# Modulation columns in steps of two weight tiles, begun one convolution pair later; chunk B's first norm in steps of two tiles

## The chip, the cores and the metric

The kernel runs on one core of one Trainium2 chip. The metric is device time in microseconds (us). Three runs of the kernel before took 1693.92, 1695.59 and 1695.64 us; the median is 1695.59 us. The profile shows one execution on the same core.

The engines are named as in the profile: PE is TensorE (PEld its weight loads), DVE is VectorE, ACT is ScalarE, POOL is GpSimd and SP is SyncE, which here issues DMAs only.

## The reference

A trunk of two layers on `x` of 1024 positions by 1024 channels, all in f32. Each layer normalises, modulates, mixes tokens, adds, and does the same around a feed-forward. The modulation comes from one vector `c`:

```python
c_act = jax.nn.silu(c)
for i in range(DEPTH):
    mod = c_act @ ada_w[i] + ada_b[i]
    sh_m, sc_m, g_m, sh_f, sc_f, g_f = jnp.split(mod, N_ADA, axis=-1)
    h = modulate(rms_norm(x, norm_mix_g[i]), sh_m, sc_m)
    ...
    x = x + (1.0 + g_m)[:, None, :] * y
    h = modulate(rms_norm(x, norm_ffn_g[i]), sh_f, sc_f)
    y = swiglu_ffn(h, ffn_w_gate[i], ffn_w_up[i], ffn_w_down[i])
    x = x + (1.0 + g_f)[:, None, :] * y
```

Layer 0 mixes by a Conformer convolution: a product to 2048 channels with a gate, a causal depthwise convolution of 31 taps, a layer norm over the channels, silu, and a product back. Layer 1 mixes by trailing means. The change is in layer 0 alone: in the vectors `g_m`, `sh_f`, `sc_f` and `g_f` of its modulation (numbered `j` = 2 to 5), and in the norm ahead of its convolution.

## The kernel before

**Tiling.** Channels lie on the 128 partitions, so 1024 channels are `KT` = 8 tiles; the 1024 positions are two chunks, A and B, of 512. Every large product is done in three parts (high by high, high by low, low by high, in `fp32r`), so one output tile of 128 channels by 512 positions takes 8 x 3 = 24 products of PE. It fills a PSUM bank, of which the tag `mm` has six.

**Order on PE.** PE executes its instructions in the order in which the Python code emits them; the other engines are ordered by a scheduler. The work stands in a list of units (`unit`, run by `run_units`). A unit emits products and calls `pace()` at fixed places: in `conv_in` after every 12 products (every 6 with `fine=2`), in the taps after every 12, in `conv_out` once behind a unit of 24. Behind each unit there is a further `pace()`, which adds nothing to PE's clock.

**The planner.** `clock` holds a planned time for PE, VectorE, GpSimd and ScalarE. `matmul` adds `n / 2400 + 0.0025` for an `fp32r` product of `n` columns and four times the first part for f32, so 12 products of 512 add 2.59. `pace()` steps the tasks that are due: first those that are urgent or `free`, then the others for as long as VectorE's or GpSimd's clock is less than 4 ahead of PE's. A task is a generator; what it yields says when it is next due. A key of `LOAD` is due so much PE clock later; `"spread"` is due 3.0 behind the later of VectorE's and ScalarE's clocks. `finish(task)` steps a task to its end and passes over what is due.

**The modulation columns.** `ada_columns(js)` (line 447) computes `js` = (2, 3) and later (4, 5), 16 weight tiles of 128 x 1024 f32 (512 KB) each time. For one tile `k` of vector `j` four products (32 columns wide, side by side in the array) take the silu of `c` as the stationary operand and the tile's four quarters as the moving one, and add to one PSUM bank. Their f32 takes two records each in the profile, eight a tile. After `k` = 7 `columns_done` copies the bank with ScalarE, yields `"spread"`, turns the row into columns with two small products (`adac`), adds the bias on VectorE and makes the gains on GpSimd. The tiles come over SP's queue into two buffers (`ADA_BUFS`); a load waits until the products that read its buffer have run. For `j = 3`, if `held[0]` is set, the turning is put off (`held_back`) to behind the first unit of `conv_out(A)`.

**Order of the units around it.** `ada_first` begins columns 2 and 3. Then stand the beginning of chunk B's norm (`norm_first`); the taps of A's pairs 0 to 3; `conv_in` for A's pairs 4 and 5, each with two banks, `a` and `g`; one unit for A's pairs 6 and 7, `finish` of B's norm, and B's 6 and 7 with the same weights; B's pairs 0 and 1; the taps that PE does itself (`pe_taps`, 46 taps, 138 products, in groups of eight whose units end at 24, 45, 69, 93, 117 and 138 products). Then:

```python
    unit(lambda take: held.__setitem__(0, True))
    unit(lambda take: finish(T["ada", 0]))
    unit(lambda take: finish(*(T["taps", 0, p] for p in range(KT) if PE_TAPS.get(p, 0) < CW)))
```

and `ada_second`, which begins columns 4 and 5; B's pairs 2, 3 and 4, beside which A's layer norm runs (products `mean`, `var` and `rstd` on PE, its sums and `v` on VectorE); `conv_out(A)` with eight units named `y`; `scale_done`, which forces `j = 4` if it isn't there; B's pair 5 beside A's norm for the feed-forward; and the feed-forward's products `p`. Behind eight of their units `first_head` finishes columns 4 and 5.

**The norm.** `norm` (line 648) takes the root of the mean of squares (`mean_rsqrt`: products `var`, small VectorE steps, products `rstd`) and then steps through the eight tiles. `modulated` emits for each tile a VectorE operation `t`, the high part `h` on ScalarE and the low part `h` on VectorE. Between two steps `pace()` may emit taps: GpSimd's and ScalarE's (`pa`, `pr`), or VectorE's (`ca`).

Of the kernel before, what the change touches and what calls it, by code (L numbers as in the profile page):

```python
# [19 lines left out]
KT = D // P  # L20
# [24 lines left out]
ADA_BUFS = 2  # L45
# [6 lines left out]

PE_TAPS = {6: 15, 7: CW}
DIAGS = 8
LOAD = {"load": 4.0, "slow": 6.0, "next": 4.0, "dots": 4.0}

ON_DVE = (1, 4)
AHEAD = 4
# [4 lines left out]
LOADED = 4  # L63
SPLIT = 2
STRAIGHT = 1
BESIDE = 12
HOLD_TAPS = 4
STRETCH = 1.2
# [63 lines left out]
def trunk(ctx, tc, xT, c, vec, ada, adan, w1f, w1, wdg, w2, wgu, wdn, wds, wpl, out):  # L132
    nc = tc.nc
    ctx.enter_context(tc.manual_schedule(engines={mybir.EngineType.PE}))
    clock = {"PE": 0.0, "V": 0.0, "G": 0.0, "S": 0.0}
# [10 lines left out]
    def matmul(out, lhsT, rhs, start, stop, more=False):  # L146
        n = out.shape[-1]
        clock["PE"] += n / 2400 * (1 if rhs.dtype == F32R else 4) + 0.0025
        last_mm[0] = nc.tensor.matmul(out, lhsT, rhs, start=start, stop=stop, skip_group_check=more).ins.name  # L149
# [55 lines left out]
    def nm(s):  # L205
        uid[0] += 1
        return f"{s}_{uid[0]}"
# [9 lines left out]
    def step(t, e):  # L217
# [8 lines left out]
        if V_.spent > before["V"] and isinstance(t, Taps) and t.ch.i:  # L226
            beside.append(V_.last.ins)
            del beside[:-BESIDE]
        for k in "VG":
# [26 lines left out]
    class Task:  # L256
# [6 lines left out]
        def step(self, e):  # L263
            if e != "V" or self.done or clock["PE"] < self.until and not forced[0]:
                return False
            try:
# [3 lines left out]
                if said == "wait":  # L270
                    return False
                if said in LOAD:
                    self.until = clock["PE"] + LOAD[said]
                elif said == "root":
# [12 lines left out]
    def block(tag, name, dt=F32R):  # L287

        pool, bufs = (raws, RAW_BUFS if tag == "raw" else ADA_BUFS) if tag in ("raw", "ada") else (slots, KT if tag[0] == "h" else KT // 2)
        return pool.tile([P, 2, 512], dt, tag=tag, name=nm(name), bufs=bufs)  # L290
# [15 lines left out]
    def bank(name):  # L306
        return ps.tile([P, 512], F32, tag="mm", name=nm(name))
# [64 lines left out]
    ccols = cst.tile([P, KT, 32], F32, name="ccols")  # L372
# [22 lines left out]
    def ada_load(src, queue=sync):  # L395
        w = raws.tile([P, D], F32, tag="ada", name=nm("adaw"), bufs=ADA_BUFS)
        queue.dma_start(w, src)
        return w
# [45 lines left out]
    Q = D // 4  # L444

    def ada_columns(js):


        todo = [(j, k) for j in js for k in range(KT)]
        src = lambda j, k: adan[k, :, (j - 2) * D : (j - 1) * D]  # L450
        ws = [ada_load(src(*t)) for t in todo[:ADA_BUFS]]
        for i, (j, k) in enumerate(todo):
            yield "load"
            if k == 0:
                acc = bank("ada")
            w = ws.pop(0)
            for g in range(4):
                matmul(acc[32 * g : 32 * g + 32, :Q], ccols[:, k, :], w[:, g * Q : g * Q + Q], start=k == 0, stop=k == KT - 1)
            clock["PE"] -= 1.3
            if i + ADA_BUFS < len(todo):  # L460
                ws.append(ada_load(src(*todo[i + ADA_BUFS])))
            if k == KT - 1 and (j != 3 or not held[0]):
                yield from columns_done(j, acc)
            elif k == KT - 1:
                held_back.append((j, acc))
# [3 lines left out]
    def columns_done(j, acc):  # L469

        rows = temp(Q)
        S_.copy(rows, acc[:, :Q])
        yield "spread"
        cols = bank("adac")
        for h in range(2):
            matmul(cols[:, 4 * h : 4 * h + 4], rows[:, h * P : h * P + P], quarters, start=True, stop=True)
        m = mod[:, j * KT : (j + 1) * KT]
        V_.tensor_tensor(m.rearrange("p (q h) -> p q h", h=2), cols[:, :KT].rearrange("p (h q) -> p q h", h=2),
                         V("ada_b", j * KT, KT).rearrange("p (q h) -> p q h", h=2), op=ADD)
        ada_gains(0, j, 0, KT, G_)  # L480
        ada_done.add((0, j))
# [148 lines left out]
    def rms(ch, keep=False):  # L630
        acc = yield from sum_sq(x[ch.i], ch.n)
        return (yield from mean_rsqrt(acc, ch.n, keep))
# [19 lines left out]
    def norm(ch, l, ffn, key, keep=False, squares=None):  # L652
        blocks = [block(f"h{ch.i}", "h") for _ in range(KT)]
        h = st[key] = [(b[:, 0], b[:, 1]) for b in blocks]
        st["blocks", ch.i] = blocks
        if squares is not None:
            rstd = yield from mean_rsqrt(squares.acc, ch.n, keep, loose=ch.i and not l)
        else:
            rstd = yield from rms(ch, keep)
        quiet[0] = ffn and not l  # L660
        for k in range(KT):
            if k == HOLD_TAPS:
                quiet[0] = False
            modulated(ch, l, ffn, h, rstd, k)
            yield


    units = []
# [1 line left out]
    def unit(emit, *weights):  # L670
        units.append((weights, emit))
# [36 lines left out]
    def conv_u(ch, p):  # L708
        u = st["u", ch.i, p] = wslot(ch, "u", p)
        if ch.i == 0:  # L710
            G_.memset(u[:, :HALO], 0.0)
        else:
            G_.tensor_copy(u[:, :HALO], uhalo[:, p, :])
        return u
# [20 lines left out]
    def conv_in(*todo, fine=4):  # L735

        def emit(take):
            got = {}
            for each in todo:
                if each is None:  # L740
                    finish(T["norm_b"])
                    continue
                ch, p = each
                conv_u(ch, p)
                wts = got.setdefault(p, [])
                b = [bank("a"), bank("g")]
                for i in range(2):
                    if len(wts) == i:
                        wts.append(take())
                    for k in range(KT):  # L750
                        products(b[i], wts[i], k, st["h", ch.i][k], k == 0, k == KT - 1)
                        if k % fine == fine - 1:
                            pace()
                conv_glu(ch, p, *b, fine < 4)
                if ch.i == 0 and PE_TAPS.get(p, 0) < CW:
                    T["taps", 0, p] = Taps(A, p)
                if ch.i == 0 and p == KT - 1:
                    for q in PE_TAPS:
                        if PE_TAPS[q] < CW:
                            split_u(q)  # L760
        tiles = list(dict.fromkeys(e[1] for e in todo if e))
        unit(emit, *[w1[p, i] for p in tiles for i in range(2)])
# [818 lines left out]
    def ending(ch, l):  # L1581
# [40 lines left out]
        def emit(parts):  # L1622
            behind_it = iter(())
            for s, (o, n) in enumerate(ENDS):
                last, straight = s == len(ENDS) - 1, []
                acc = st["upper"][:, o : o + n]
                for d in range(KT // 2):
# [7 lines left out]
                    S_.activation(sq, xs, AF.Square)  # L1635
                    if last and d > STRAIGHT:
                        straight.append(sq)
# [53 lines left out]
    for k in range(KT):  # L1691
# [4 lines left out]
        if k > 1:  # L1696
            acc = squares[0]
# [16 lines left out]
    w = ada_pair(0)  # L1714
# [7 lines left out]
    for k in range(KT + 1):  # L1722
        if k < KT:
            if k:
                w = ada_pair(k)
# [3 lines left out]
                dots = [V_.last.ins]  # L1729
# [8 lines left out]
        if k < KT:  # L1738
# [7 lines left out]
            t = temp(A.n) if k else first_t  # L1746
# [48 lines left out]
    def ada_first(take):  # L1795
        T["ada", 0] = Task(ada_columns((2, 3)), False, 0)
        T["ada", 0].free = True
    unit(ada_first)
    def norm_first():
        squares = Squares(B, True)  # L1800
        for k in range(KT + 1):
# [7 lines left out]
    taps(A, *range(FIRST))  # L1809
    for p in range(FIRST, KT - 1 - SHARE):  # L1810
        conv_in((A, p))
    some = range(KT - 1 - SHARE, KT)
    conv_in(*[(A, p) for p in some], None, *[(B, p) for p in some])
    put("ln_a", lambda: layer_norm_silu(A), True)
# [227 lines left out]
```

## Time and profile before

| What | us |
|---|---|
| median of three runs | 1695.59 |
| the profiled execution | 1694.43 |
| its span in the profile | 1692.7 |
| PE busy | 1665.5 |
| columns 2 and 3 on PE, first to last tile | 71.64 to 173.63 |
| columns 4 and 5 on PE, first to last tile | 206.14 to 323.01 |
| the 32 tiles' own products on PE | 20.4 |
| chunk B's norm: `rstd` on PE | 101.58 |
| first product of B's pair 6, which reads that norm | 118.37 |

All times but the first two are counted from the start of the span, which is 1.7 us shorter than the execution. A line of the timeline gives the start, the time taken, the engine, the source line, the operation, `out<-in` by the program's names, the operand's shape and the count of merged instructions, and in brackets the engine's idle time before it with what ended that. `L149` and `L126` are the helpers that emit all products and all vector operations, so the tiles' names tell the work: `ada<-adaw,ccols` is a modulation tile, `a` and `g` are the banks of a convolution pair, `tap` the taps on PE, and `first` the first four pairs.

### The profile page before, as it was taken

The page shows a single profiled execution, that of the slowest core. Times are in us where ns is not written, and L with a number is a line of the kernel's source. Part 1 is how long each engine was busy: PE and PEld are TensorE (multiplying, and loading weights), DVE is VectorE, ACT ScalarE, POOL GpSimd, SP SyncE. Part 2 cuts the span into 40 slices and gives each one's busy share as a digit, 9 for nine tenths or more (in the row PEclk, how much of TensorE's full clock was granted, in tenths as well). Part 3 has the DMA queues.
Part 4 walks back from the last instruction along what each step waited for, and adds up shares of the span by engine and source line. Part 5 has one row for each costly group of instructions (what it writes and reads, how often), then busy time and mean ns, then how long its engine had stood idle before and what let it go on. Part 6 is the DMA issues. An engine that isn't in the chain of part 4 may idle for free.

```text
span 1692.7 us, 21280 instructions
## 1 busy us (share of the span) xinstructions
PE 1665.5 (98%) x7586; PEld 1356.0 (80%) x7586; DVE 1318.3 (78%) x1872; ACT 799.7 (47%) x1085; POOL 489.6 (29%) x566
## 2 busy tenths in 40 slices
PE   7999999999999999999999999999999999999997
PEld 5777777778887888888888888888888888888887
DVE  8889899899758887888665797848877677668656
ACT  3679686866546332333213436646422222234344
POOL 3587767796001111212110222100111111000013
PEclk9999999999999999999999999999999999999999
DMA  8958987828675789886878846877677776677564
GB/s 302 289 173 234 231 232 200 224 78 238 216 237 155 257 261 298 271 265 212 339 266 285 260 146 202 245 243 212 175 231 230 213 221 193 203 269 206 190 168 125
DMA packets 115884, 380.70 MB, mean 225 GB/s; under 512 B 12289, under 2 KB 14465, under 8 KB 115778
## 3 DMA queue, kind: packets, MB, share of 16 engines
q1 hardware_dynamic: 78464, 247.99, 41.6%
q0 software_dynamic: 36736, 130.83, 31.6%
q8 instruction: 60, 0.98, 0.2%
q10 hardware_dynamic: 578, 0.53, 0.1%
q14 instruction: 46, 0.38, 0.1%
HBM read 311.92 MB, written 63.18 MB: 222 GB/s over the span
## 4 chain that ended last, share of the span: by engine, by line
PE 87%; DVE 6%; DMA 2%; issue 2%; ACT 2%; POOL 1%; DVEq 0%; SPq 0%; ACTq 0%; POOLq 0%
PE a L149 24%; PE dn L149 23%; PE e L149 13%; PE p L149 12%; PE y L149 6%; PE g L149 3%; PE first L149 3%; PE tap L149 2%; POOL pa L126 1%; PE ada L149 1%; DVE t L126 1%; DMA adaw<-in_adan_dram 1%; DVE x L126 1%; PE var L149 1%; DVE w L126 1%
## 5 line engine op out<-in xcount | busy, mean ns | idle before, releaser
L126 ACT CAST w<-raw 128x1024 fp32r<-128x1024 f32 (+1 forms) x249 | 258.8, 1042 | 329.8 <-PE dn L149 93.6
L149 PE MATMUL dn<-g,w 128*128 128x512 f32 x1152 | 265.3, 390 | 1.6 <-DVE g L126 1.0
L149 PEld LDWEIGHTS dn<-g,w 128*128 128x128 f32 x1152 | 215.5, 188 | 48.0 <-DVE g L126 1.3
L126 DVE TENSOR_TENSOR w<-raw,w 128x1024 fp32r<-128x1024 f32 (+1 forms) x177 | 217.7, 1233 | 42.8 <-ACT w L126 42.4
L149 PE MATMUL a<-n,w 128*128 128x512 f32 x1056 | 247.7, 390 | 1.1 <-DVE n L126 0.7
L149 PE MATMUL p<-h,w 128*128 128x512 f32 x1056 | 244.2, 390 | 0.8 <-DVE h L126 0.6
L126 POOL TENSOR_TENSOR pa<-pa,pr 128x512 f32<-128x512 f32 x160 | 229.6, 1521 | 23.3 <-ACT pr L126 17.1
L149 PEld LDWEIGHTS a<-n,w 128*128 128x128 f32 x1056 | 197.8, 188 | 44.2 <-DVE n L126 2.2
L149 PEld LDWEIGHTS p<-h,w 128*128 128x128 f32 x1056 | 197.3, 188 | 43.8 <-DVE h L126 1.5
L149 PE MATMUL dn<-hi,w 128*128 128x512 f32 (+1 forms) x600 | 173.7, 373 | 0.8 <-DVE w L126 0.8
L126 DVE SCALAR_TENSOR_TENSOR ca<-u,vecs,ca 128x512 f32<-128x512 f32 x245 | 169.7, 746 | 0.5
L126 DVE SCALAR_TENSOR_TENSOR x<-dn,gains,x 128x512 f32<-128x512 f32 (+1 forms) x144 | 100.8, 729 | 35.7 <-PE dn L149 35.4
L149 PEld LDWEIGHTS dn<-hi,w 128*128 128x128 f32 x600 | 109.7, 188 | 20.9 <-DVE w L126 1.3
L149 PE MATMUL a<-t,w 128*128 128x512 f32 x528 | 123.5, 389 | 0.8 <-DVE w L126 0.8
L149 PE MATMUL e<-b,w 128*128 128x512 f32 x528 | 123.4, 389 | 0.6 <-DVE r L126 0.6
L149 PE MATMUL e<-t,w 128*128 128x512 f32 x528 | 123.3, 389 | 0.0
L126 ACT ACTIVATE pr<-u,vecs 128x512 f32<-128x512 f32 x160 | 108.2, 716 | 25.5 <-POOL pa L126 17.4
L1119 POOL DMA_DIRECT2D raw<-in_wgu_dram x41 | 36.3, 886 | 285.7 <-DVE k L126 89.8
L149 PEld LDWEIGHTS a<-t,w 128*128 128x128 f32 x528 | 99.0, 188 | 21.8 <-DVE w L126 1.2
L149 PEld LDWEIGHTS e<-b,w 128*128 128x128 f32 x528 | 99.0, 188 | 21.6 <-DVE r L126 1.0
L149 PEld LDWEIGHTS e<-t,w 128*128 128x128 f32 x528 | 99.1, 188 | 20.6
L149 PE MATMUL dn<-lo,w 128*128 128x512 f32 (+1 forms) x300 | 111.7, 372 | 0.0
(183 smaller groups left out, 2374.3 us busy)
## 6 DMA issues: line engine op xcount, KB each, us to landing
raw<-in_wgu_dram SPq DMA_DIRECT2D x132, 512.0 KB, 4.9
adaw<-in_ada_dram POOLq DMA_DIRECT2D x48, 512.0 KB, 7.4
raw<-in_wdn_dram SPq DMA_DIRECT2D x44, 512.0 KB, 7.8
raw<-in_wgu_dram POOLq DMA_DIRECT2D x41, 512.0 KB, 7.0
raw<-in_w_dram SPq DMA_DIRECT2D x36, 512.0 KB, 6.1
gd<-g POOLq DMA_DIRECT2D x36, 512.0 KB, 7.8
g<-gd SPq DMA_DIRECT2D x36, 512.0 KB, 5.5
kinds<-k POOLq DMA_DIRECT2D x33, 512.0 KB, 7.2
```

The costliest lines, as they stand in the source:

```text
L126: self.last = self.order(getattr(self.eng, name)(out, *args, **kw))
L149: last_mm[0] = nc.tensor.matmul(out, lhsT, rhs, start=start, stop=stop, skip_group_check=more).ins.name
L1119: d = order(nc.gpsimd.dma_start(w[i], wgu[l, fp, src], accum_op=ADD))
```

## The change

Three things change. `ada_columns` takes its tiles by twos: it waits once, does the eight products of two tiles one after the other, and then issues the loads of the next two together. It is due 16.0 of PE's clock after its beginning (`"first"`) and 11.0 after each step (`"both"`), where it was 4.0 for each tile (`"load"`); a pair's net price in PE's clock falls from 2 x (1.717 - 1.3) to 2 x (1.717 - 1.465). The unit `ada_first` moves from ahead of B's norm to behind A's pair 4. And `norm` yields after every second tile for chunk B in layer 0, so that two tiles are emitted in one step.

```diff
-LOAD = {"load": 4.0, "slow": 6.0, "next": 4.0, "dots": 4.0}
+LOAD = {"load": 4.0, "both": 11.0, "first": 16.0, "slow": 6.0, "next": 4.0, "dots": 4.0}
...
+WHEN = 4
...
         ws = [ada_load(src(*t)) for t in todo[:ADA_BUFS]]
-        for i, (j, k) in enumerate(todo):
-            yield "load"
-            if k == 0:
+        for i in range(0, len(todo), ADA_BUFS):
+            yield "both" if i else "first"
+            these = todo[i : i + ADA_BUFS]
+            if these[0][1] == 0:
                 acc = bank("ada")
-            w = ws.pop(0)
-            for g in range(4):
-                matmul(acc[32 * g : 32 * g + 32, :Q], ccols[:, k, :], w[:, g * Q : g * Q + Q], start=k == 0, stop=k == KT - 1)
-            clock["PE"] -= 1.3
-            if i + ADA_BUFS < len(todo):
-                ws.append(ada_load(src(*todo[i + ADA_BUFS])))
+            for (j, k), w in zip(these, ws):
+                for g in range(4):
+                    matmul(acc[32 * g : 32 * g + 32, :Q], ccols[:, k, :], w[:, g * Q : g * Q + Q], start=k == 0, stop=k == KT - 1)
+                clock["PE"] -= 1.465
+            ws = [ada_load(src(*t)) for t in todo[i + ADA_BUFS : i + 2 * ADA_BUFS]]
             if k == KT - 1 and (j != 3 or not held[0]):
                 yield from columns_done(j, acc)
...
             modulated(ch, l, ffn, h, rstd, k)
-            yield
+            if not ch.i or l or k % 2:
+                yield
...
-    unit(ada_first)
...
         conv_in((A, p))
+        if p == WHEN:
+            unit(ada_first)
```

## The prediction

> **What bounds the kernel now.** I read the page first, then the waits of TensorE (PE) in the first 330 us, where all the changed code runs, then PE's timeline there.
>
> ```profile
> PE 1665.5 (98%) x7586; PEld 1356.0 (80%) x7586; DVE 1318.3 (78%) x1872; ACT 799.7 (47%) x1085; POOL 489.6 (29%) x566
> PE var L149 <- DVE acc L126: 5.8, 1, 5.8
> ...
> PE p L149 <- DVE h L126: 0.6, 2, 0.3
> PE ada L149 <- DMA adaw<-in_adan_dram: 0.6, 1, 0.6
> PE y L149 <- DVE v L126: 0.5, 1, 0.5
> ```
>
> PE is busy for 98% of the span, and after the first 20 us its waits (waited for, total, times, longest) are tenths. So PE's instruction list is the clock of the kernel: what leaves that list is gained and what enters it is paid, unless the list then meets a wait. Three such places stand close by: the modulation tile that waited 0.6 us for its DMA, the first `y` unit (0.5 us for VectorE's `v`), and the first `p` units (0.6 us for `h`).
>
> **One tile, and two in one step.** Today each weight tile is a step of its own behind 24 products.
>
> ```profile
> 91.03 0.64 PE L149 MATMUL ada<-adaw,ccols 128*32 128x256 f32 x8 [0.60 <-DMA adaw<-in_adan_dram]
> 91.59 1.05 PE L149 MATMUL var<-ones,acc 128*128 128x1 f32 x8
> ...
> 101.58 1.05 PE L149 MATMUL rstd<-ident,col 128*128 128x128 f32 x8
> ...
> 117.80 0.64 PE L149 MATMUL ada<-adaw,ccols 128*32 128x256 f32 x8
> 118.37 5.74 PE L149 MATMUL a<-h,w 128*128 128x512 f32 x24
> 123.95 0.50 PE L149 MATMUL adac<-quarters,t 128*128 128x4 f32 x4
> 124.31 5.69 PE L149 MATMUL g<-h,w 128*128 128x512 f32 x24
> ```
> ```profile
> 247.62 5.68 PE y L149 x24
> 253.30 0.57 PE ada L149 x8
> 253.87 16.55 PE y L149 x72
> ```
> ```profile
> L149 PE MATMUL ada<-adaw,ccols x256: 379/391/403, 71.6 to 323.3; 128*32 128x256 f32 x128
> ...
>   issue: 11.0, 31
> ```
>
> Both `y` runs of the chain follow a tile, so 48 more products cost 16.55 - 5.68 = 10.87, 0.2265 us each. 24 then need 5.44, and 5.68 holds 0.24 of restart. A tile costs 0.57 + 0.24 = 0.81 us. The x256 are 8 records a tile: 32 tiles, 25.9 us. The eight run in two rounds; 0.64 of busy time less 0.39 for the last one leaves 0.25 between rounds. The last row is weight loads sitting idle before tiles, 11.0 us in 31 times, 0.35 each: the list empties at the change of shape. In a pair the second tile has the same shape, so I give it two rounds, 0.50, and none of the emptying: a pair is 0.81 + 0.50 = 1.31, and 16 pairs save 16 x 0.31 = 5.0 us. No row shows two tiles in a row. At the dear end the second pays the full 0.81 (gain 0); at the cheap end its rounds hide in the first's 0.39 tail, 0.39 less each, 11.2 in all. I take 0.31, nearest to the rows of one tile.
>
> [...]
>
> **Where the pairs fall.** The kernel places steps by its own PE clock. 12 products add 2.59 to it and end in a look at what is due; a pair adds 0.50, `var` 0.02, `rstd` 0.86. Zero is the end of A's pair 4, where the loads are now begun. The first step is due at 16.0 and comes at 18.15 (half of A6's `g`). Each next is due 11.0 behind: 29.87 (half of A7's `g`), 43.33 (end of B6), 56.78 (half of B0's `a`). That ends shift `j = 2`; its turning into columns waits by the clocks of VectorE and ScalarE, three looks (7.8), 65.07. The fifth is then due at 76.07, just past the end of B1 (75.43), and falls 12 products into the taps (78.0), the sixth at 69 (90.6), the seventh, due at 102.06, misses the look at 117 products (101.1) and comes at 129 of 138. The eighth isn't due at all: `finish(T["ada", 0])` forces it at 138. Its two tiles can be fetched only when the seventh has left the two buffers. **So nine products separate a pair from the loads of the next**, where the loads used to have a whole bank. One look less for the columns gives 21 products, one more gives none.
>
> **Up to the forced pair.**
>
> ```profile
> 173.63 0.64 PE L149 MATMUL ada<-adaw,ccols 128*32 128x256 f32 x8
> 174.20 7.75 PE L149 MATMUL tap<-us,w 128*128 128x496 f32 x33
> 181.79 0.51 PE L149 MATMUL adac<-quarters,t 128*128 128x4 f32 x4
> 182.15 18.61 PE L149 MATMUL tap<-us,w 128*128 128x508 f32 x81
> 200.60 5.61 PE L149 MATMUL a<-h,w 128*128 128x512 f32 x24
> 206.14 0.64 PE L149 MATMUL ada<-adaw,ccols 128*32 128x256 f32 x8
> 206.71 1.13 PE L149 MATMUL mean<-acc,ones 128*128 128x512 f32 x2
> ```
>
> Before 200.60 go: 16 tiles, 12.96; the DMA wait, 0.60, since early pairs are 11 units apart; the second `adac`, 0.36 (123.95 to 124.31), which moves behind the first `y`. Seven pairs, 9.17, come. Gain 4.75: the taps end at 195.85 and the seventh pair 9 x 0.2265 = 2.04 earlier, at 193.8.
>
> ```profile
> 192.77 0.33 SPq L491 DMA_DIRECT2D raw<-in_w_dram  x1
> 193.15 1.01 SPq L167 DMA_DIRECT2D adaw<-in_adan_dram  x2
> ```
> ```profile
> DMA to landing us min/median/max: 8.5/9.6/10.8
> ```
> ```profile
> DMA to landing us min/median/max: 3.4/5.9/12.4
> ```
> ```profile
> 0.00:20.00 20.00, 8.38 (x21) 5.01 (x21) 12.83 (x28) 10.11 (x17) 2.77 (x38) 1.00 0.91 347
> ```
>
> SP issues two at 193.15 today, in this very stretch, behind a weight load; they land 8.5 and 10.8 us after issue. The third row is all 32 loads; 3.4 alone plus 512 KB at the best rate seen, 347 GB/s, 1.5, makes 4.9 the short end, 10.8 the long one. I take 8.0, between them, as the change's weight load comes about 2 us sooner and is half done. On SP nothing but the next weight loads queues behind these two, five tiles ahead of PE. The second is issued by 194.4 and lands at 202.4; 0.5 later the pair is done, 202.9 (199.8 to 205.7). PE waits some 6 us. With 5.54 for the bank, `mean` begins at 208.4 (205.3 to 211.2) against 206.71: **1.7 us late** (1.4 early to 4.5 late).
>
> **From there to the end.**
>
> ```profile
> 203.99 1.49 DVE L126 TENSOR_TENSOR acc<-acc,u 128x512 f32<-128x512 f32 x2
> ...
> 228.36 4.87 DVE L126 TENSOR_TENSOR u<-u,rstd 128x512 f32<-128x512 f32 x8 [0.17 <-PE rstd L149]
> ...
> 245.58 0.68 DVE L126 TENSOR_TENSOR v<-t,v 128x512 fp32r<-128x512 f32 x1
> ```
> ```profile
> 301.66 0.64 PE L149 MATMUL ada<-adaw,ccols 128*32 128x256 f32 x8
> ```
>
> Columns 4 and 5 begin at the same place as before, their first step due 16 later. Between `mean` and `var` one pair replaces two tiles, +0.31; between `var` and `rstd` one tile goes, +0.81. From `rstd` to the last product of the first `y`, VectorE works 228.36 to 246.26 without a hole, so a saving there only lengthens the 0.5 us wait: 0. Behind it 10 tiles and two `adac` (8.82) become 6 pairs and three (8.94), -0.12. The tile at 301.66 stood ahead of the `h` waits and no pair replaces it there: they grow, -0.81. Sum +0.2. After 340 us nothing is edited, and PE's list is what it was.
>
> **Chunk B's norm.** Its root is one look later (end of A6's `g`), because PE's clock lacks the old steps; in time that is 101.2 against 101.58.
>
> ```profile
> L126 DVE SCALAR_TENSOR_TENSOR h<-t,mod,h 128x512 fp32r<-128x512 f32 x8 | 9.7, 1224 | 0.0
> L126 DVE SCALAR_TENSOR_TENSOR t<-x,gains,rstd 128x512 f32<-128x512 f32 x8 | 5.7, 737 | 2.7 <-PE rstd L149 2.7
> ...
> L126 DVE SCALAR_TENSOR_TENSOR u<-a,vecs,t 128x512 f32<-128x512 f32 x1 | 0.7, 739 | 0.0
> ...
> L126 DVE SCALAR_TENSOR_TENSOR uhalo<-a,vecs,t 128x30 f32<-128x30 f32 x1 | 0.2, 230 | 0.0
> ```
>
> That is VectorE from the root's columns (102.7) to the norm's end (122.75): 20.1 us, 15.4 of them the norm's sixteen operations, the rest gating and taps. B6 starts at 118.37 now; with two pairs ahead in place of eight tiles, and the DMA wait gone, at 113.9. It reads the last tile 21 products in, 4.8 later, 118.7: 17.5 behind the root, whose spreading takes 0.9. Two tiles at a time put four at the root and two at each of the next steps, so little but the gating (0.9) can stand between: 16.3 of 16.6, no cost. If as much stands between as today, PE waits 20.1 + 0.9 - 17.5 = 3.5; that end stays in the range. The taps put off are still due only at the taps' `finish`.
>
> **What else moves.**
>
> ```profile
> 129.49 7.46 ACT L126 ACTIVATE x<-x,gate_b 128x512 f32<-128x512 f32 x12
> ```
>
> Shift `j = 2` ends some 25 us later in PE's list, and with it POOL's two small gains and this block on ScalarE, which needs them. Behind it queue the sigmoids that free PE's banks; PE has one bank's time, 5.5, in hand, so 0 to 2.0, and I take 0, as no wait on PE followed it here. The first two loads leave SP's queue at 62 and come about 12 us later, where 4 loads fewer are in flight by 98; PE waited for none but its tile, so 0. The accumulator of `j = 3` stays in its bank past the taps; if the six run out, a bank's release by VectorE costs tenths to 1 us. The smaller price in the clock gives VectorE some 5 us less planned work by 340 us, all of it due later.
>
> **Sum.** 1.7 - 0.2 = 1.5 us slower. The profiled execution took 1694.43 (span 1692.7), 1.2 under the median of 1695.59; I add to the median: **1697.1**, no change that can be seen.
>
> **Rivals.** *The forced pair costs nothing* (it is reached later than I count, or its loads land at once). PE would be at `mean` at 195.85 + 1.31 + 5.54 = 202.7, where VectorE's `acc` ended at 205.48 and can come earlier only by what it idled: gain 1.2 to 4.0, with the 0.2 a time of 1691.4 to 1694.2. For it: three steps miss the look before by 0.64 of the clock alone, so one term that I left out undoes the replay. Against: the same count puts the old tiles where the trace has them, one behind each 24 products. *PE runs slow after the wait*, the other side:
>
> ```profile
> 11.88 1.87 PE L149 MATMUL var<-ones,acc 128*128 128x1 f32 x8 [5.85 <-DVE acc L126]
> ```
> ```profile
> 19.28 4.94 PE L149 MATMUL first<-h,w 128*128 128x512 f32 x12 [1.65 <-ACT h L126]
> ```
>
> After 5.85 us idle the eight `var` took 1.87 us where 1.05 is the rule, and 12 products took 4.94 against 2.72: 2.2 lost, though the granted clock of that stretch reads 1.00. A wait of 6 us at 196 would be like it; 1.5 + 2.2 = 3.7 slower, 1699.3. [...] *The pair saves nothing*: seven pairs put the forced load 2.2 later and the rest adds 2.5: 6.2 slower, 1701.8.
>
> **Chances.** A measurement tells 0.2%, 3.4 us, from no change. Forecast 0.51 (1694.0 to 1699.9 by the loads, to 1703 with a wait at B6: 0.02 faster, 0.37 same, 0.12 slower); free forced pair 0.30 (0.17 faster, 0.13 same); slow PE 0.12 (0.05 same, 0.07 slower); no saving 0.07 (0.01 same, 0.06 slower). Together 0.19, 0.56, 0.25. The range, 1691.2 to 1702.5, leaves out the ends of the outer cases.
>
> **What would show it.** Right: groups of 16 `ada` products about 0.5 longer than 0.64; none with a DMA wait before 130 us; a wait for `adaw` of 4 to 9 us right behind the last tap; a longer wait of the first `y`. Wrong: an eighth pair without a wait, `mean` before 205, `var` or taps slowed behind the wait, or B6's `a` waiting for `h`.

## The result: 1.8% slower, and the profile after

The changed kernel takes 1726.12 us (median of six runs, 1725.01 to 1729.54) against 1695.75 for the kernel before in the same job: ratio 1.0181, 95% interval 1.0171 to 1.0192. The prediction, 1697.1 with a range to 1702.5, missed by 29 us; "slower" had been given 0.25. The profiled execution took 1725.4, its span is 1723.6.

The engines' shares on the page show nothing of it: PE still has 97%.

```profile
PE 1672.0 (97%) x7586; PEld 1366.4 (79%) x7586; DVE 1317.7 (76%) x1872; ACT 802.3 (47%) x1088; POOL 487.9 (28%) x566
```

PE's waits between 60 and 370 us do (waited for: total, times, longest). Before, the rows of this view that lie in the edited stretch came to 1.7 us (`p` 0.6, `ada` 0.6, `y` 0.5).

```profile
PE ada L150 <- DMA adaw<-in_adan_dram: 6.0, 2, 5.2
PE adac L150 <- ACT t L127: 4.7, 1, 4.7
PE y L150 <- ACT t L127: 4.6, 1, 4.6
PE rstd L150 <- DVE col L127: 4.3, 1, 4.3
PE p L150 <- ACT t L127: 2.6, 1, 2.6
PE g L150 <- ACT t L127: 1.6, 2, 1.4
PE a L150 <- DVE h L127: 1.6, 2, 0.8
PE p L150 <- DVE h L127: 1.3, 2, 0.9
```

That is 26.7 us, 25.0 more than before. PE's timeline of the changed kernel shows what each wait leaves behind:

```profile
107.39 2.05 PE L150 MATMUL rstd<-ident,col 128*128 128x128 f32 x8 [4.30 <-DVE col L127]
...
109.10 7.37 PE L150 MATMUL a<-h,w 128*128 128x512 f32 x24
116.30 2.88 PE L150 MATMUL g<-h,w 128*128 128x512 f32 x12
119.11 1.07 PE L150 MATMUL ada<-adaw,ccols 128*32 128x256 f32 x16
120.12 3.06 PE L150 MATMUL g<-h,w 128*128 128x512 f32 x12
123.01 4.47 PE L150 MATMUL a<-h,w 128*128 128x512 f32 x19
...
142.78 5.60 PE L150 MATMUL g<-h,w 128*128 128x512 f32 x24
148.22 2.88 PE L150 MATMUL a<-h,w 128*128 128x512 f32 x12
...
203.49 1.07 PE L150 MATMUL ada<-adaw,ccols 128*32 128x256 f32 x16
...
211.96 1.08 PE L150 MATMUL ada<-adaw,ccols 128*32 128x256 f32 x8 [5.20 <-DMA adaw<-in_adan_dram]
213.84 1.08 PE L150 MATMUL ada<-adaw,ccols 128*32 128x256 f32 x8 [0.81 <-DMA adaw<-in_adan_dram]
214.85 4.65 PE L150 MATMUL a<-h,w 128*128 128x512 f32 x12
219.34 1.02 PE L150 MATMUL mean<-acc,ones 128*128 128x512 f32 x2
...
259.51 7.28 PE L150 MATMUL y<-v,w 128*128 128x512 f32 x24 [4.63 <-ACT t L127]
271.45 1.01 PE L150 MATMUL adac<-quarters,t 128*128 128x4 f32 x4 [4.67 <-ACT t L127]
272.32 7.63 PE L150 MATMUL y<-v,w 128*128 128x512 f32 x24
...
354.69 4.61 PE L150 MATMUL p<-h,w 128*128 128x512 f32 x12 [2.58 <-ACT t L127]
```

Three things are to be seen. **The pairs cost what was forecast**: from 116.30 to 123.01 lie 24 products and a pair, 6.71; 24 products alone take 148.22 - 142.78 = 5.44; a pair is 1.27 (forecast 1.31). **The eighth pair waited as forecast**, 5.20 + 0.81 = 6.0. **And after each long wait the products run slow**: `rstd` 2.05 for 1.05, `a` 7.37 for 5.60, half a bank 4.65 for 2.88, `y` 7.28 and 7.63 for 5.60, `p` 4.61 for 2.88. The forced pair itself takes 2 x 1.08 where a pair has 1.07. That is 1.0 + 1.8 + 1.8 + 1.7 + 2.0 + 1.7 + 1.1 = 11.1 us, behind five waits.

So 25 us of waits and 11 of slow products, less what PE's shorter list gives. The same product starts later than before by these amounts (us, profile against profile; negative is earlier): A7's `a` 3.2, first tap 3.8, B2's `a` 14.3, first `y` 19.0, second `y` 24.8, `p` at 343 us of before 31.7, last product 30.8. All of it is lost ahead of 345 us. 25.0 + 11.1 - 30.8 leaves 5.3 that the list did give (forecast 5.0); the pairs paid, and the waits with the slow products took it nearly seven times over.

### The profile page after: what moved, and what is told of

Its sections match the earlier page's. It is cut to its first block, busy times and chain, and to the rows that moved or that the text cites. A ratio compares the mean times of both kernels' runs of the same rounds, so it can differ in the third digit from the quotient of the medians.

```text
span 1723.6 us, 21288 instructions
## 1 busy us (share of the span) xinstructions
PE 1672.0 (97%) x7586; PEld 1366.4 (79%) x7586; DVE 1317.7 (76%) x1872; ACT 802.3 (47%) x1088; POOL 487.9 (28%) x566
## 4 chain that ended last, share of the span: by engine, by line
PE 82%; DVE 5%; ACT 3%; DMA 3%; issue 1%; POOL 1%; DVEq 0%; ACTq 0%; POOLq 0%
PE dn L150 24%; PE a L150 21%; PE e L150 13%; PE p L150 12%; PE y L150 7%; PE tap L150 2%; PE g L150 1%; DMA raw<-in_w_dram 1%; DVE ca L127 1%; DVE t L127 1%; ACT t L127 1%; PE ada L150 1%; POOL pa L127 1%; ACT w L127 1%; DVE h L127 1%
## 5 line engine op out<-in xcount | busy, mean ns | idle before, releaser
L127 POOL TENSOR_TENSOR pa<-pa,pr 128x512 f32<-128x512 f32 x161 | 225.8, 1465 | 31.5 <-ACT pr L127 28.0
```

The source lines that it names most:

```text
L127: self.last = self.order(getattr(self.eng, name)(out, *args, **kw))
```

## The experiments

Each ratio is to the kernel before in the same job, with its 95% interval; the times are medians. 0.1% is 1.7 us.

**The eighth pair and the first loads (e1, e2, e7).** e1 begins the loads where the kernel before does, and makes the first pair due so much later (26.36) that the pairs stand where they do in the changed kernel. e2 makes the pairs of `j` = 2 and 3 due every 9.0, so the eighth comes by itself ahead of the taps' end and nothing is held back. e7 does both.

```diff
-            yield "both" if i else "first"
+            yield "both" if i else "late" if js[0] == 2 else "first"                  # e1, "late": 26.36, and unit(ada_first) ahead of norm_first
+            yield ("sooner" if js[0] == 2 else "both") if i else "first"              # e2, "sooner": 9.0
+            yield ("both" if i else "first") if js[0] != 2 else "sooner" if i else "late"   # e7, and the unit ahead
```

> The changed kernel with one thing undone: the first two tiles are again fetched ahead of A's pair 4 (due 26.36 of PE's clock later, so that every pair stands where the change puts it). Theory 1 (the delay comes in separate waits, the first of them a weight load that queued 5.7 us behind the two tiles at 70 us and held ScalarE for 7.2 us): ScalarE's wait for a weight near 84 to 91 us falls under 2 us, rstd doesn't wait over 1 us (4.3 now), the a bank behind it takes 5.6 us and not 7.4; 7 to 10 us are won, about 1717; the waits behind the last tap and at the first y stay. Theory 2 (the planner's new price of a pair has put VectorE's and ScalarE's work in a worse order, whatever the loads do): within 3 us of the changed kernel, 1723 to 1729.

> The changed kernel with columns 2 and 3 due 9.0 of PE's clock behind each step (11.0 in the change), so that the eighth pair falls inside the taps and isn't forced at their end; columns 4 and 5 as in the change. Theory 1: no wait for adaw behind the last tap (6.0 us now), no wait for the copied row of j = 3 behind the first y (4.7 us now), and the slow products behind both are gone (some 1.8 us each): 12 to 16 us won, 1710 to 1714, with the waits near 107 us as in the change. Theory 2: the waits move elsewhere, within 4 us of the changed kernel, 1722 to 1730.

> The loads at the old place (as in the first experiment) and columns 2 and 3 due 9.0 behind each step (as in the second) together. If their gains are separate: the second's 1702 less the 6 us by which the first stood ahead at 345 us, 1694 to 1698. If the first's gain is lost in a later wait, because VectorE's sum of A's taps doesn't come sooner: 1700 to 1703, with mean waiting for acc.

e1: 1723.88, ratio 1.0175 (1.0144 to 1.0206). The wait of `rstd` and its slow products are gone: the first tap starts 3.5 earlier than before, where it was 3.8 later, and the lead over the changed kernel is 6.3 us at 343 us. 6 us of it go again at 1050 us, in layer 1, where nothing was edited: `var` waits 1.9 there for VectorE, and the mean granted clock of the profile is 0.988, where the changed kernel's is 0.990. The profile is of the slower of e1's two executions (1726.03 and 1721.72), so it isn't shown that each of them loses this; e6 loses as much there, also in the slower of two, and e11 some 4. e2: 1702.08, ratio 1.0041 (1.0025 to 1.0057). Taking the forced pair away is worth 1.40%, 23.7 us; with a step every 9.0 the pairs ahead of it come sooner too. e7: 1698.53, ratio 1.0015 (1.0006 to 1.0025); on top of e2 the early loads are worth 0.26%, 4.4 us (about 1 to 8, by the two intervals).

Why two loads cost so much shows in the changed kernel's timelines. The first fence has SP's issues, the second ScalarE's work, the third VectorE's:

```profile
69.89 1.95 SPq L168 DMA_DIRECT2D adaw<-in_adan_dram  x2
73.21 25.68 SPq L492 DMA_DIRECT2D raw<-in_w_dram  x5
```
```profile
90.76 1.05 ACT L127 CAST w<-raw 128x1024 fp32r<-128x1024 f32 x1 [7.23 <-DMA raw<-in_w_dram]
...
95.34 0.69 ACT L127 ACTIVATE t<-g,vecs 128x512 f32<-128x512 f32 x1 [0.73 <-POOL pa L127]
```
```profile
96.06 0.75 DVE L127 SCALAR_TENSOR_TENSOR u<-a,vecs,t 128x512 f32<-128x512 f32 x1 [8.26 <-ACT t L127]
...
97.54 0.16 DVE L127 TENSOR_SCALAR col<-var 128x4 int32<-128x4 int32 x1
...
107.09 0.16 DVE L127 SCALAR_TENSOR_TENSOR col<-var,col 128x4 f32<-128x4 f32 x1
```

The weight issued at 73.21, behind the two tiles, landed at 90.66, 17.5 us later; the like of it before took 12.0 (72.94 to 84.93). ScalarE's cast stood waiting for it 7.23 us, and behind it in ScalarE's order the sigmoid `t` of the bank that was ready. VectorE (third fence) waited 8.26 for that sigmoid, began B's root at 97.54 and had it at 107.25, and PE's `rstd` stood. Nothing waited for the tiles themselves. How much this costs differs from run to run: in five others with the two loads at this place (e2, e5, e6, e11, e16) that weight took 12.1 to 14.9 us and `rstd` waited 0.8 to 3.6, so the changed kernel's profile, with 17.5 and 4.3, shows the dearest case; in e1 the weight took 6.9.

**What the eighth pair costs by (e5, e6).** e5 copies the row of `j = 3` out of its bank at once and holds back the copy. e6 fetches no tiles for the eighth pair, which multiplies those of the seventh again: a part of the modulation isn't computed, all work on PE is.

```diff
             elif k == KT - 1:
-                held_back.append((j, acc))
+                rows = tmp.tile([P, Q], F32, tag="rows", name=nm("rows"), bufs=1)
+                S_.copy(rows, acc[:, :Q])
+                held_back.append((j, acc, rows))                                     # e5
...
-            ws = [ada_load(src(*t)) for t in todo[i + ADA_BUFS : i + 2 * ADA_BUFS]]
+            if js[0] != 2 or i + 2 * ADA_BUFS < len(todo):
+                ws = [ada_load(src(*t)) for t in todo[i + ADA_BUFS : i + 2 * ADA_BUFS]]   # e6
```

> The changed kernel, but ScalarE copies the finished row of j = 3 right behind the forced pair, into a tile of its own, and not when its turning into columns is emitted behind the first y. Theory A (PE waits there for a copy that queues on ScalarE behind a square of the first y's own result): the 4.7 us wait of adac is gone and the y bank behind it takes 5.6 us and not 7.6; 5 to 8 us won, 1718 to 1721; the 4.6 us wait at the first y stays. Theory B (PE would only wait for something else there): under 2 us won.

> The changed kernel, but the eighth pair of columns 2 and 3 multiplies the seventh pair's tiles again, so nothing is fetched for it (that part of the modulation isn't computed). Every product keeps its place. Theory A (the fetch is what the forced pair costs, and PE's list sets the end): the 6.0 us of waits and about 2 us of slow products go, 8 us won, 1718. Theory B (VectorE's sum of A's taps, ready at 214.9 where mean begins at 219.3, is close behind): at most 4.5 us won there, and mean waits for acc; 1721 to 1723.

e5: 1716.41, ratio 1.0127 (1.0107 to 1.0147). Both waits on ScalarE are gone, that of `adac` and that of the first `y`, and the time is 0.54%, 9.2 us, less. Not all of that is theirs: e5's profile is 4.9 us ahead of the changed kernel's at the first tap already, ahead of anything that the edit touches, since `rstd` waited 0.8 there. From B2's `a` to the fifth `y` it gains another 5.5; waits of 2.7 and 1.2 for VectorE and 0.8 for GpSimd at `y` stand in place of the two. That the first `y`'s wait for ScalarE went too says what it had waited for: the bank. In the changed kernel ScalarE's order there is

```profile
257.47 1.28 ACT L127 ACT_TABLE_LOAD   x1
258.77 0.69 ACT L127 ACTIVATE t<-g,vecs 128x512 f32<-128x512 f32 x1
...
266.82 1.05 ACT L127 CAST w<-raw 128x1024 fp32r<-128x1024 f32 x1 [2.07 <-PE y L150]
...
271.05 0.35 ACT L127 COPY t<-ada 128x256 f32<-128x256 f32 x1
```

The held accumulator keeps one bank, so `y` needs the bank of a `g` whose sigmoid stands behind a table load; and the copy of the held row is emitted behind the first `y`, into a queue in which ScalarE is late: PE reached `adac` at 266.8 and got its row at 271.4.

e6: 1725.48, ratio 1.0180 (1.0160 to 1.0201). The wait for the fetch is gone and the time can't be told from the changed kernel's. PE then reaches `mean` earlier and stands there, in e6's timeline:

```profile
204.12 1.07 PE L150 MATMUL ada<-adaw,ccols 128*32 128x256 f32 x16
205.12 3.01 PE L150 MATMUL a<-h,w 128*128 128x512 f32 x12
211.35 2.07 PE L150 MATMUL mean<-acc,ones 128*128 128x512 f32 x2 [3.22 <-DVE acc L127]
```

The first two rows follow each other without a wait; 3.22 us at `mean` and slow products take the place of the 6.0. At 343 us e6 is 4.7 ahead of the changed kernel, 2.6 of which it had at the first tap, where its `rstd` waited 2.9; so 2.1 are left for the fetch. Its profile loses 6 us at 1050 us, as e1's does.

**Parts of the change alone (e3, e4, e9, e11, e12).** e3 undoes the move only; e4 takes single tiles, with move and norm as changed; e9 is the kernel before with the norm by two; e12 the kernel before with the pairs; e11 the changed kernel with the norm by one.

```diff
+    unit(ada_first)                                   # e3: here, ahead of norm_first, and not behind pair 4
...
-            if not ch.i or l or k % 2:
-                yield
+            yield                                     # e11
```

> The changed kernel with the columns begun at their old place (the move undone; steps of two tiles and the norm by twos stay). All pairs fall some 10 of PE's clock earlier, so the eighth isn't forced. Theory 1: the waits at rstd, behind the last tap and for the row of j = 3 are all gone, 20 to 26 us won, 1700 to 1706; with no other cost it comes to the gain that the pairs were sized at, 1691. Theory 2: 1715 or more.

> The changed kernel with one tile a step, 4.0 of PE's clock apart, as before the change, but begun behind A's pair 4, and with the norm by twos. Theory 1: the two first loads still queue ahead of weights at 70 us, so a wait of rstd of 1 to 4 us stays, but no pair is forced: 1698 to 1706. Theory 2 (the pairs are to blame): within 3 us of the kernel before, 1693 to 1699.

> The kernel before, with only chunk B's first norm by two tiles a step. Theory A (every run with the norm by twos has VectorE wait 3 to 5 us for GpSimd's part of A's last taps near 200 us, so the norm's taps put off are the cause): that wait appears here, the last sum of A's taps ends at 207 to 209 (205.5 before), 1697 to 1701. Theory B (the norm by twos is harmless by itself): 1694 to 1697 and the sum by 206.

> The changed kernel with the norm by one tile a step, all else as changed. The forced pair and the held row stay, so 1718 to 1727 in either theory; by theory A the sum of A's taps ends 3 us sooner than 214.9 and the wait behind B6's first products grows.

> The kernel before with only the steps of two tiles, begun at the old place (first step due 16.0, then 11.0), the norm by one. If the 0.31 us a pair comes through: 1689 to 1692. If VectorE's and ScalarE's chain takes what PE's list wins, as in every run so far: 1694 to 1701, with PE's waits up by about what the list lost.

e3: 1704.06, ratio 1.0053 (1.0030 to 1.0075). e12: 1704.75, 1.0055 (1.0038 to 1.0072). e4: 1697.59, 1.0007 (0.9995 to 1.0018). e9: 1697.88, 1.0017 (1.0007 to 1.0027). e11: 1729.61, 1.0203 (1.0183 to 1.0223). So the pairs lose by themselves, 0.5%, at the old place too; the move with single tiles costs nothing that can be told (no tile is forced there; the one new wait is 3.1 us for ScalarE, behind the same two loads); the norm by two costs 0.1 to 0.3% alone; what it gains beside the pairs (0.11% from e10, below, to e7, 0.22% from e11 to the changed kernel) is not told from nothing by the intervals.

Where the pairs lose is best seen in e7, which has no forced pair and no late load. PE's waits in its stretch from 60 to 370 us come to 9.6 us, where the kernel before has 1.7. Its PE timeline at the first unit that reads B's norm, and PE's granted clock there (in the second fence: window, its length, busy time and count of PE, PEld, DVE, ACT and POOL, then the clock, the DMA share and GB/s):

```profile
118.70 0.49 PE L150 MATMUL a<-h,w 128*128 128x512 f32 x1 [0.33 <-ACT h L127]
120.48 0.96 PE L150 MATMUL a<-h,w 128*128 128x512 f32 x3 [1.29 <-DVE h L127]
122.18 1.22 PE L150 MATMUL a<-h,w 128*128 128x512 f32 x2 [0.73 <-DVE h L127]
123.20 3.81 PE L150 MATMUL g<-h,w 128*128 128x512 f32 x12
```
```profile
120.00:124.00 4.00, 2.79 (x7) 1.98 (x8) 4.00 (x5) 3.14 (x6) 3.61 (x4) 0.72 0.00 0
```

PE had come to B6 4 us earlier than before and met the norm: 2.35 us of waits, and 12 products of `g` that take 3.8 for 2.9. The lead of 4.0 at A7's `a` is 1.5 at the first tap, though on the way four pairs (5.1) stand in place of nine tiles and should have made it 6.1. The rest goes in a wait of 1.3 for the seventh pair's tiles, among the taps, and at `mean` (1.7 in e7, 1.8 in e12, 3.4 in e3): VectorE's last sum of A's taps ended at 205.5 before, and at 207.7, 210.6 and 209.4 in these.

**Why VectorE's sum is late (e8, e10).** Two causes were thought of: the pair's smaller price in the planner's clock, and the norm by two. e8 is e7 with the old price, e10 is e7 with the norm by one.

```diff
-                clock["PE"] -= 1.465
+                clock["PE"] -= 1.3                    # e8
```

> The kernel of the seventh experiment with the old price of a tile in PE's planning clock (1.3 taken off and not 1.465), so that the planner gives VectorE and GpSimd 0.33 more per pair. Theory A (the cheaper price leaves A's last taps to the forced finish, which deals them to GpSimd, and VectorE waits 3 to 5 us for its part): that wait of VectorE near 200 us falls under 2 us, the last sum of A's taps ends 2 to 4 us sooner, 1691 to 1695. Theory B (the order of the taps doesn't hang on so little): within 1.5 us of the seventh.

> The seventh experiment's kernel (pairs, loads early, no forced pair) with the norm by one tile a step. Theory A: VectorE's wait for GpSimd near 195 us falls under 1.5 us, the last sum of A's taps ends by 205, 1692 to 1695. Theory B: within 1.5 us of the seventh's 1698.5; the gain of the pairs is met by other waits.

e8: 1701.19, ratio 1.0039 (1.0025 to 1.0053). e10: 1699.85, 1.0026 (1.0017 to 1.0035). Neither made the sum earlier: it ended at 208.5 and 209.1. PE waits 1.7 at `mean` in e10 too, and 0.4 in e8, where `mean` stands 12 products later in its list. Both theories fell.

**ScalarE's sixteen additions (e13 to e16).** The traces showed another candidate. Once the gains of `j = 2` are there, ScalarE adds `gate_b` to the sixteen tiles of `x`. Before, that was at 129.49. In e7 the row comes later, and so does the block, in one piece (first fence, ScalarE); a weight load of GpSimd waits 10 us for the cast behind it (second fence, POOL), and GpSimd's taps `pa`, which VectorE's sum needs, queue behind that load:

```profile
151.60 9.91 ACT L127 ACTIVATE x<-x,gate_b 128x512 f32<-128x512 f32 x16
...
161.99 1.03 ACT L127 CAST w<-raw 128x1024 fp32r<-128x1024 f32 x1
```
```profile
164.38 0.89 POOL L498 DMA_DIRECT2D w<-in_wdg_dram  x1 [9.97 <-ACT w L127]
165.01 4.38 POOL L127 TENSOR_TENSOR pa<-pa,pr 128x512 f32<-128x512 f32 x3
```

e13 is e7 with the block held back; e15 the kernel before, and e16 the changed kernel, with the same hold (in these three, and in e18 below, the unit that emits A's additions also moves behind `need("ln_a")`, where A's layer norm is finished); e14 is the kernel before with the block held until B7 is gated, so that it falls where e7 has it.

```diff
             S_.activation(x[ch.i][k], x[ch.i][k], AF.Identity, bias=gate_b[:, k : k + 1])
+            tc.add_manual_dep(S_.last.ins, st["last_update" if ch.i else "last_sq"], edge, reason="behind the sums")   # e13, e15, e16
+            tc.add_manual_dep(S_.last.ins, st["b7"], edge, reason="behind the gate")                                   # e14
```

> The kernel of e7 (early loads, no forced pair), whose loss against before is 2.8 us, with ScalarE's sixteen additions x<-x,gate_b held back: A's eight behind the last sum of squares of A's layer norm, B's eight behind A's last update of x. In e7 they stand at 151.60 in one piece of 9.91 us, and GpSimd's load of w waits 9.97 us for ScalarE's cast behind them, with the taps pa queued behind that load. Theory (the later row j=2 moves this block into the stretch of the taps, and through ScalarE's casts and GpSimd's queue it makes VectorE's last sum late): no GpSimd wait of over 5 us between 145 and 170, VectorE's last sum of A's taps at 206 or sooner (207.7 in e7), mean waits under 0.5 (1.7), and the time falls to 1694.0 to 1696.5. Rival (PE is sooner, and VectorE's own work sets the sum): last sum at 207 or later, 1697.5 to 1699.5. A third case: the block hurts at its new place, beside v, and y waits over 2 us.

> The kernel before, PE's list untouched, with only the sixteen additions x<-x,gate_b held back until B's last pair of the shared unit is gated (about 152 us in place of 129.5). Theory (the block's place alone costs): GpSimd's load of w waits 5 to 10 us for ScalarE's cast, VectorE's last sum of A's taps ends at 207 to 210 (205.5 before), mean waits 1 to 4 us, and the time is 1697.5 to 1701. Rival (it is the pairs that do it): last sum within 1 us of 205.5, 1695 to 1696.5.

> The kernel before with the sixteen additions held back as in e13. Theory: they cost little where they stand in before (ScalarE has free time by 137), so nothing is gained at the taps; 1694.5 to 1697. If GpSimd's taps were held by them here too: last sum before 204, but PE gets to mean at 206.7, so 1695 or more all the same. A case on the other side: they collide with v and y, 1697 to 1700.

> The changed kernel with the sixteen additions held back as in e13. In the changed kernel they stand at 164.3 to 178, and GpSimd's product waits 5.3 us for ScalarE there. Theory: VectorE's last sum falls from 214.9 to 208 to 212, but PE still waits for the eighth pair (until 213.8) and for ScalarE at y and at the held row, so little of it is seen: 1721 to 1726. Rival (the same cause as in e7 is the larger part here as well): 1716 to 1720.

e13: 1701.71, ratio 1.0041 (1.0028 to 1.0054). The sum ends at 205.3 and GpSimd's longest wait for a cast is 3.8: that step of the theory held. PE, sooner itself, still waits 1.7 at `mean`, and the time got worse: 5 us were lost behind 290 us, where B's eight additions now stood. e14: 1701.91, 1.0045 (1.0032 to 1.0057), the sum at 211.8 and 5.3 us at `mean`. That is about the loss forecast, but not by the way forecast, as the row of VectorE in e14 says:

```profile
135.11 11.63 DVE L126 TENSOR_TENSOR acc<-u 128x512 f32<-128x512 f32 x1
146.66 8.64 DVE L126 SCALAR_TENSOR_TENSOR ca<-u,vecs,ca 128x512 f32<-128x512 f32 x13
```
```profile
135.87 5.63 POOL L126 TENSOR_TENSOR pa<-pa,pr 128x512 f32<-128x512 f32 x4
140.87 1.47 POOL L497 DMA_DIRECT2D w<-in_w_dram  x1
141.48 4.67 POOL L126 TENSOR_TENSOR pa<-pa,pr 128x512 f32<-128x512 f32 x3
```

A sum of 512 columns that takes 0.69 us before took 11.63, without a wait. With the block gone from 129 to 137, GpSimd (second fence) had its `pr` in time and ran seven additions one behind the other, to 146.15; VectorE's sum ended 0.6 later. e15 has the same row, 11.64, and no block near it: 1712.44, ratio 1.0103 (1.0087 to 1.0118). e16: 1724.53, 1.0173 (1.0159 to 1.0187); the sum ends at 208.1 in place of 214.9, but PE waits for the eighth pair and for ScalarE all the same.

**The stall by itself, and half the block (e17, e18).** In e17 the first sum of e14 has one operand in PSUM: ScalarE copies it there. e18 is e13 with only A's eight additions held back.

```diff
+            if k == 1 and not ch.i:
+                S_.copy(acc, was)
+                was = acc
             V_.tensor_tensor(acc, was, vs[k], op=ADD)                                                        # e17
...
+            if ch.i == 0:
+                tc.add_manual_dep(S_.last.ins, st["last_sq"], edge, reason="behind the sums")                # e18
```

> The kernel of e14, whose first sum of A's taps (acc<-u, two operands in SBUF) took 11.63 us where it takes 0.69 before, while GpSimd ran seven additions pa<-pa,pr without a hole and ended them at 146.15, 0.5 before the sum. Here ScalarE copies the first operand into the bank and VectorE adds the other to it (one operand in SBUF, one in PSUM, as the later sums have it); the work is the same but for one copy of 0.57. Theory (the sum was held off by GpSimd's run of additions, and that is the 6.9 us of e14): the sum takes 0.7 to 1.0, the last sum of A's taps ends at 204 to 208, mean waits under 1.5 us, 1695 to 1698. Rival (the additions at 145 cost by themselves, as first thought for e14): last sum at 209 or later, 1699 to 1702.

> The kernel of e13 with only A's eight additions held back (behind the last sum of squares) and B's eight free to go where they went in e7 (about 150 us, now one piece of some 5 us). Theory (e13 gained 2.4 us at the last sum and lost it again behind 290 us, where B's additions stood in one piece ahead of the norm's values): the last sum ends at 205 to 206.5, the loss behind 290 is gone, 1695 to 1697.5. Rival (what e13 lost behind 290 us is PE's own lead running into VectorE's norm, whatever the additions do): 1699 to 1702.

e17: 1696.28, ratio 1.0008 (0.9999 to 1.0017); the sum takes its usual time again and nothing waits at `mean`, though GpSimd again runs its seven additions without a hole (140.39 to 150.66). So the stall was the loss of e14, as far as the intervals tell, and the block at 150 us by itself costs nothing that can be told in the kernel before:

```profile
140.92 0.68 DVE L126 TENSOR_TENSOR acc<-acc,u 128x512 f32<-128x512 f32 x1
```

e18: 1696.75, ratio 1.0008 (0.9999 to 1.0017). The last sum ends at 206.0 (207.7 in e7), and the loss behind 290 us is gone, so in e13 that was the additions' new place. No version beat the kernel before.

**The account.** Ratios in a row: changed kernel 1.0181; no forced pair 1.0041 (e2); loads early too 1.0015 (e7); A's additions late too 1.0008 (e18). In us, at 17 to the per cent: 23.7 for the forced pair with what follows it, of them 5 to 9 for the held accumulator (e5) and some 2 for the fetch (e6), while no run takes the other 12 to 16 apart; 4.4 for the place of two loads; 1.2 for ScalarE's block, which the intervals of e7 and e18 do not fully part from nothing; 1.4 (none to 2.9) that pairs cost even so.

## Why the prediction was wrong

**Right:** the price of a pair (1.27 for 1.31), the place of all eight pairs, the 6.0 us for the forced one, no wait for a tile ahead of 130 us. Sizes on PE's own list held, and so did the emptying once a step: the weight loads of the modulation tiles sat idle, without a wait that the profile shows, 14 times for 16 pairs, 5.0 us in all, and 31 times for 32 single tiles before, 11.0.

**"PE's instruction list is the clock of the kernel"** is the step that failed first. It was read from 98% busy and waits of tenths. The waits were tenths because the other chains ended just behind PE, not because they had room: VectorE's norm of B ended at 122.81, 0.2 before the product that reads its last tile, and its last sum at 205.48, 1.2 before `mean`. A shorter list ran into them (e7, e12), and none of its 5 us came out. The first rival had this in one place, `mean`, and still gave it a gain.

**"The first two loads leave SP's queue at 62 and come about 12 us later ... PE waited for none but its tile, so 0"**: 4.4 us (e7 against e2), and 8.5 in the changed kernel's profile up to A7's `a` (1.45 + 4.30 of waits, 1.0 + 1.8 of slow products), the dearest of six. The step asked who waits for the tiles; it should have asked what queues behind them. SP's queue was counted for the forced pair, not for the first.

**"The accumulator of `j = 3` stays in its bank past the taps; ... a bank's release by VectorE costs tenths to 1 us"**: 5 to 9 us (e5). The bank was released by ScalarE, behind a table load, and the copy of the row queued behind ScalarE's backlog, a wait that the prediction did not have at all.

**B's norm, "16.3 of 16.6, no cost"**: waits of 0.83 and 0.73 in the changed kernel, 2.35 plus slow products in e7. The prediction kept up to 3.5 in its range; the term was mis-sized by about 2 to 4.

**"PE runs slow after the wait"** was a rival with one price, 2.2, and a chance of 0.12. In the changed kernel it came true behind every wait of 2.6 us or more from 60 to 370 us: five waits, 11.1 us. The prediction put against it that the granted clock read 1.00 in the first 20 us; the trace of the kernel before has no record of the clock ahead of 23.0 us, so that 1.00 says nothing. Where there are records, a short window shows the fall. The changed kernel, in three windows (columns as above):

```profile
203.00:209.00 6.00, 3.75 (x28) 2.18 (x26) 1.47 (x3) 3.37 (x5) 6.00 (x8) 1.00 1.05 321
...
212.00:216.00 4.00, 3.19 (x19) 1.31 (x20) 2.62 (x4) 0.00 (x0) 1.28 (x1) 0.50 1.04 273
216.00:220.00 4.00, 4.00 (x14) 2.99 (x12) 0.00 (x0) 0.00 (x0) 0.00 (x0) 0.70 0.71 282
```

The clock is 1.00 over 203 to 209 us, in which the wait of 5.20 begins, and 0.50 and 0.70 over the 8 us behind it. Behind the other four it reads 0.50 as well: over 107 to 111 (a wait of 4.30), 260 to 262 (4.63), 272 to 276 (4.67) and, behind the wait of 2.58 at `p`, 356 to 358.

**What a long forced wait was worth** came out differently from both the forecast and the account of the waits: without the fetch (e6) some 2 of the 6.0 us and the slow products come out, since VectorE's sum is later still. Most of what the eighth pair costs lies elsewhere: in its accumulator, and in a part that stays open.

**Open:** 12 to 16 of the 23.7 us that go with the forced pair; the 6 us that e1 and e6 lose at 1050 us; and why VectorE's last sum of A's taps is no earlier in e18 (206.0) than before (205.5), though PE leads by 4 us at A7's `a`.

## What to carry to other kernels

An engine at 98% with waits of tenths is not proof of room in the others: before a list is shortened, look how long ahead of each wait its releaser ended, for a shorter list gains no more than that there. A step that moves counts with everything it puts ahead of others: two loads on busy DMA engines (share 0.96 over 70 to 80 us in the changed kernel) and a row that stays in a bank cost more here than the work that was saved. And a wait on TensorE cost more than itself here: the five of 2.6 to 5.2 us in the changed kernel had 1.7 to 2.9 us of slow products behind each, 11.1 in all.

## What the runs showed of the hardware

**A VectorE sum held off by GpSimd.** The sum of two operands in SBUF took 11.63 and 11.64 us (e14, e15) beside an unbroken run of seven GpSimd additions, 0.69 beside an idle GpSimd (the kernel before, at 139.2), and 0.68 with one operand in PSUM (e17). The profile shows it as the sum's own time, not as a wait. In e14 and in e15 the sum ended 0.6 us behind the last of the seven additions; it did not get in between two of them.

**The clock fell behind short waits too**: in e7, with waits of 0.33, 1.29 and 0.73 from 118 to 122 us, it reads 1.00 over 116 to 120, 0.72 over 120 to 124 and 0.86 over 124 to 128. A single wait of 1.45 in the changed kernel (for `g`, at 96.08) showed no fall: the clock reads 1.00 over 96 to 105, and the next 12 products took 3.03, where 12 behind a pair take 3.06.
